# Where four tiles lie and who prepares the last norm: a one-core encoder block

## The chip, the core and the metric

The kernel runs on one core of a Trainium2 chip. The metric is the device time of one execution in microseconds (us), and of several executions the median. Engines are named as in the profile: PE (TensorE), DVE (VectorE), ACT (ScalarE), POOL (GpSimd), SP (SyncE, which here only issues DMAs).

## The reference

One layer on 1024 tokens of width 1024, in float32. Two mixers share an input projection: sparse attention (8 heads of 64, each query keeps the 256 best keys by an index score) and gated linear attention. Their outputs go through `w_out`, a residual and a first layer norm. Then 32 experts, of which each token takes two, a residual and a second layer norm.

```python
mix = jnp.concatenate([ya, yb], axis=-1) @ w_out[l]
h = layer_norm(DEEPNORM_ALPHA * h + mix, ln1_g[l], ln1_b[l])
ffn = hier_moe(h, ...)            # 32 experts, top 2 of one group of 8
h = layer_norm(DEEPNORM_ALPHA * h + ffn, ln2_g[l], ln2_b[l])
```

## The kernel before

**Projections.** x lies in SBUF as high and low halves (`xhi`, `xlo`), so that three fast matmuls make one float32 product. `load_w` brings each piece of `w_in` in as `wraw` and splits it into `whi` and `wlo`. The last projection is `values(1, ...)`: four matmul groups, each copied by ScalarE from PSUM into a tile `vs` (L687) and written by a DMA of GpSimd's queue to the DRAM tensor `d_av` (L688). The `vs` tiles take turns in buffers of two tags, `vs` and `wraw`.

**Attention.** For each of four head pairs and eight query blocks of 128 (item n = 8 * pair + block) and for both heads: PE makes scores `s` (L839), DVE adds the bias and takes the maximum into `Sm` (L844), ACT takes the exponential (L852), PE transposes `Sm` into PSUM `pt` (L863), and ACT or DVE copies that to SBUF as `PT` (L868, L866). A block later PE multiplies `PT` with the values into `ot` (L877). PE's order runs: scores of n, transposes of n-1, products of n-2. Every four blocks the sums' reciprocals are spread by POOL into `rb` (L910), transposed by PE (L885), copied by ACT into `R` (L887), multiplied by DVE (L888) and written to `d_mix` by SP (L889). The order on PE, ACT and DVE here is that of the code.

The SBUF pool `att` of `Sm`, `PT`, `rb`, `R` is opened where the projections' pools have been closed. A tile that is allocated over closed tiles waits for whatever last used the bytes, a DMA that reads them among it. A tag with `bufs=2` takes its place at its first two allocations, in the order in which the code asks.

**Experts.** 192 pieces of weights of 1 MB go through 13 slots, eight of the pool `big`, two in the score buffer `sc`, three more; SP issues each when its slot is free. `results` scales an expert's two output halves by the gate, one on ACT (L1404) and one on DVE (L1405), and an indirect DMA adds the rows to `d_y` (L1406). After the 32 experts a loop of 0 to 16 turns takes care of overfull experts; here it turns zero times, but all engines and DMAs meet in front of it (L1501).

**Last norm.** `last_norm` loads eight tiles `r` of `d_y` (L1560, SP), while PE spreads gain and shift over 128 partitions in four PSUM banks (L1332). [...] `LAST` has a word of three letters for each tile: first who takes the statistics (A: ACT with two passes, L1574 and L1577; D: DVE with `bn_stats`, L1583), then for each half who applies them (D: DVE alone, L1604 and L1605; P: ACT scales at L1607, then POOL multiplies and adds at L1612; G and S: DVE and POOL share, L1610 and L1612). The reciprocal root is POOL's (`rstd`, L498 and L499). SP writes the results (L1614, L1616).

Of the kernel before, what the change touches and what calls it, by code (L numbers as in the profile page):

```python
# [9 lines left out]
F32 = mybir.dt.float32  # L10
# [5 lines left out]
AF = mybir.ActivationFunctionType  # L16
OP = mybir.AluOpType
# [4 lines left out]
D = 1024  # L22
# [7 lines left out]
NE = 32  # L30
# [17 lines left out]
WORAW = 4  # L48


LAST = ("ADP", "DDD", "APP", "DDD", "ADD", "ADD", "ADD", "AGS")
WS = [(t + 1) * 128 for t in range(2, NT)]
SOFF = [int(v) for v in np.cumsum([0] + WS)]

# [110 lines left out]
class Kern:  # L165
# [514 lines left out]
    def values(self, g, w, tiles, queue=None):  # L680
        nc = self.nc
        queue = queue or nc.sync
        for t in tiles:

            vs = self.wpool.tile([128, 2, 2, 128], F32, name="vs", tag="wraw" if g and t > 2 else "vs", bufs=3 if g and t > 2 else 2)
            ps = yield from self.proj_n_steps(w, t)
            nc.scalar.copy(vs, ps.rearrange("p t (a b) -> p a t b", a=2))  # L687
            queue.dma_start(self.d_av[g][:, :, t:t + 2, :].rearrange("a p t c -> p a t c"), vs)  # L688
# [131 lines left out]
    def attention(self, p, before):  # L820

        nc = self.nc
        ident = self.c["ident"]
        items = [(hp, t) for hp in range(4) for t in range(NT)]
        st = {}

        def scores(n, hd):
            s = st[n]  # L830
            t, W = s["t"], s["W"]
            qq, kk, _ = s["loads"]
            lq = qq[:, hd, t * 128:(t + 1) * 128]
            ps = self.bank("s", [128, 2 * 512])
            cuts = [(0, W)] if W <= 512 else [(0, W // 2), (W // 2, W // 2)]
            for c, (c0, m) in enumerate(cuts):
                mm = max(m, 256)
                for a in range(2):
                    nc.tensor.matmul(ps[:, 512 * c:512 * c + mm], lq, kk[hd][:, a, c0:c0 + mm], start=a == 0, stop=a == 1)  # L839

            Sm = p.tile([128, T], F32, name="Sm", bufs=4)
            mx = p.tile([128, 1], F32, name="mx", bufs=4)
            m = cuts[0][1]
            nc.vector.tensor_tensor_reduce(  # L844
                Sm[:, :W].rearrange("p (c m) -> p c m", m=m), ps.rearrange("p (c m) -> p c m", m=512)[:, :len(cuts), :m],
                self.bias[t][:, :W].rearrange("p (c m) -> p c m", m=m), -0.125, -OUTSIDE, op0=OP.add, op1=OP.min, accum_out=mx)
            s["S"].append((Sm, mx))

        def weights(n, hd):
            s = st[n]  # L850
            Sm, mx = s["S"][hd]
            nc.scalar.activation(Sm[:, :s["W"]], Sm[:, :s["W"]], AF.Exp, bias=mx, scale=-1.0,  # L852
                                 accum_out=s["rec"][:, s["t"] % 4, hd:hd + 1])

        def turned(n, hd):
            s = st[n]
            t, P = s["t"], s["S"][hd][0]
            PT = p.tile([128, NT, 128], F32, name="PT", bufs=4)
            for b0 in range(0, t + 1, 4):
                nb = min(4, t + 1 - b0)  # L860
                pt = self.bank("pt", [128, 512])
                for b in range(nb):
                    nc.tensor.transpose(pt[:, 128 * b:128 * b + 128], P[:, 128 * (b0 + b):128 * (b0 + b) + 128], ident)  # L863
                o = PT[:, b0:b0 + nb, :].rearrange("p a b -> p (a b)")
                if b0 or (t < 4 and hd):
                    nc.vector.tensor_copy(o, pt[:, :128 * nb])  # L866
                else:
                    nc.scalar.copy(o, pt[:, :128 * nb])  # L868
            s["PT"].append(PT)

        def mixed(n):
            s = st.pop(n)
            t, v, ot = s["t"], s["loads"][2], s["ot"]
            for b in range(t + 1):
                for hd in range(2):
                    r = slice(64 * hd, 64 * hd + 64)
                    nc.tensor.matmul(ot[r, t % 4, :], v[:, b, r], s["PT"][hd][:, b, :], start=b == 0, stop=b == t)  # L877
            if t % 4 == 3:
                return s

        def shares(s):

            rp = self.bank("pt", [128, 4, 128])
            for i in range(4):
                nc.tensor.transpose(rp[:, i, :], s["rb"][:, 2 * i:2 * i + 2, :].rearrange("p a b -> p (a b)"), ident)  # L885
            R = p.tile([128, 4, 128], F32, name="R", bufs=2)
            nc.scalar.copy(R.rearrange("p a b -> p (a b)"), rp.rearrange("p a b -> p (a b)"))  # L887
            nc.vector.tensor_mul(R, R, s["ot"])  # L888
            nc.sync.dma_start(self.d_mix[s["t"] // 4][:, :, s["hp"], :].rearrange("t p q -> p t q"), R)  # L889

        rec = ot = done = None
        with self.tc.manual_schedule(engines={mybir.EngineType.PE, mybir.EngineType.Activation, mybir.EngineType.DVE}):
            for n in range(len(items) + 2):
                new, turn = n if n < len(items) else None, n - 1 if 0 < n <= len(items) else None
                if new is not None:
                    hp, t = items[n]
                    loads = before(n)
                    if t % 4 == 0:
                        rec = p.tile([128, 4, 2], F32, name="rec", bufs=2)
                    st[n] = {"hp": hp, "t": t, "W": 128 * (t + 1), "S": [], "PT": [], "rec": rec, "loads": loads}  # L900
                if turn is not None:
                    s = st[turn]
                    if s["t"] % 4 == 0:
                        ot = self.bank("ot", [128, 4, 128])
                    s["ot"] = ot
                    if s["t"] % 4 == 3:
                        rb = s["rb"] = p.tile([128, 8, 64], F32, name="rb", bufs=2)
                        rr = p.tile([128, 8], F32, name="rr", bufs=2)
                        nc.vector.reciprocal(rr, s["rec"].rearrange("p a b -> p (a b)"))
                        nc.gpsimd.tensor_copy(rb, rr.unsqueeze(2).to_broadcast([128, 8, 64]))  # L910
                for hd in range(2):
                    if new is not None:
                        scores(new, hd)
                    if turn is not None:
                        turned(turn, hd)
                    if new is not None:
                        weights(new, hd)
                over, done = done, mixed(n - 2) if n > 1 else None
                if over:
                    shares(over)  # L920
            shares(done)
# [415 lines left out]
    def expert_stream(self, cols, x, work):  # L1337


        nc = self.nc  # L1340
# [15 lines left out]
        def second(e, a, between=None):  # L1356
            ys = [self.bank("ot", [128, 512]) for _ in range(2)]
            product(a, ys, 4, 0)
            ahead()
            out = between() if between else None  # L1360
            product(a, ys, 4, 1)
            self.results(ys, cols(e))
            ahead()
            return out

# [2 lines left out]
        for e in range(NE):  # L1368
# [25 lines left out]
                x = self.rows_in(self.xg[(e + 1) % 2], cols(e + 1)[0]) if e else x1  # L1394
            if e:
                last = second(e - 1, ah, (lambda: self.turn_act(act)) if e == NE - 1 else None)
        second(NE - 1, last)

    def results(self, ys, cols):

        nc = self.nc
        tok, gate = cols
        y = self.ep.tile([128, D], F32, name="y", bufs=2)
        nc.scalar.activation(y[:, :512], ys[0], AF.Copy, scale=gate)  # L1404
        nc.vector.tensor_scalar(y[:, 512:], ys[1], gate, None, op0=OP.mult)  # L1405
        nc.gpsimd.indirect_dma_start(out=self.d_y, out_offset=bass.IndirectOffsetOnAxis(ap=tok.bitcast(U32), axis=0),  # L1406
                                     in_=y, in_offset=None, bounds_check=T - 1, oob_is_err=False, compute_op=OP.add)

# [145 lines left out]
    def last_norm(self, gain, shift):  # L1554
        nc = self.nc
        with self.pool("last") as p:
            rs, fs = [], []
            for t in range(NT):
                r = p.tile([128, D], F32, name="r", bufs=NT)
                nc.sync.dma_start(r, self.d_y[t * 128:(t + 1) * 128])  # L1560
                rs.append(r)


            both = p.tile([128, 2, D], F32, name="both")
            for i, ps in enumerate((gain, shift)):
                for k in range(2):
                    nc.scalar.copy(both[:, i, 512 * k:512 * k + 512], ps[k])

            def stats(t):

# [20 lines left out]
            for t in range(NT):  # L1591
# [9 lines left out]
                for k in range(2):  # L1601
# [4 lines left out]
                    else:  # L1606
                        nc.scalar.activation(r[:, s], r[:, s], AF.Identity, scale=f[:, 2:3], bias=f[:, 3:4])  # L1607
                        for i, (ps, op) in enumerate(((gain, OP.mult), (shift, OP.add))):
                            if kinds[k] == "GS"[i]:
                                nc.vector.tensor_tensor(r[:, s], r[:, s], ps[k], op=op)  # L1610
                            else:
                                nc.gpsimd.tensor_tensor(r[:, s], r[:, s], both[:, i, s], op=op)  # L1612
                    if t == NT - 1:
                        nc.sync.dma_start(self.out[t * 128:(t + 1) * 128, s], r[:, s])  # L1614
                if t < NT - 1:
# [15 lines left out]
```

## Time and profile before

| | |
|---|---|
| median of 3 runs | 1294.08 us (1291.38 to 1295.2) |
| the profiled execution | 1292.31 us, span 1290.5 us, mean granted clock 0.97 |
| busy in the span | PE 93%, DVE 80%, ACT 61%, POOL 31% |
| attention | first scores 393.24 us, first output product (L1057) 525.49 us |
| experts | last matmul ends at 1247.8 us |
| last norm | first load issued at 1259.42 us, last output issued at 1286 us |

The profile's page shows where PE is busy and which chain of work ended last. A list of waits names who held whom up; a timeline shows the instructions of a stretch. "x4" is a count of equal instructions merged into a row.

### The profile page before, as it was taken

Reading aid. Unit: us, or ns where it says so; the run is one execution under the profiler, and the core shown is the slowest. Engines: PE = TensorE matmul, PEld = TensorE weight load, DVE = VectorE, ACT = ScalarE, POOL = GpSimd, SP = SyncE. Lnnn points to the kernel's source line nnn. Section 1 sums busy time; section 2 is a strip of 40 time slices with the busy share of each in tenths; the row PEclk is TensorE's granted clock in tenths of the full one; section 3 lists DMA queues with packets and bytes.
Section 4 is the critical chain, followed back from the end, with each engine's and each line's share of the span. In section 5 each row is a group of like instructions: output and inputs, shape, how many; then the busy total and the mean of one; then the engine's idle time right before and its main releaser. Section 6 shows DMA issues by size and latency. Waiting matters only on the chain.

```text
span 1290.5 us, 19395 instructions
## 1 busy us (share of the span) xinstructions
PE 1204.2 (93%) x6926; PEld 1003.1 (78%) x6926; DVE 1028.6 (80%) x1657; ACT 792.8 (61%) x1112; POOL 394.5 (31%) x354
## 2 busy tenths in 40 slices
PE   6999999999996999999859999999999999999962
PEld 5979988877795888888747888888888888888851
DVE  4567897999993666477768999889998899889945
ACT  4378366665534667132257777777777777777835
POOL 2532642345753453011121321112221222122215
PEclk9999999999998999999979999999999999999985
DMA  7653544325468661874378999999999999999926
GB/s 257 163 180 99 191 156 126 112 61 143 105 186 242 190 170 58 308 278 164 131 271 313 375 372 367 382 368 360 380 365 369 351 361 357 352 356 353 321 44 260
DMA packets 133588, 322.61 MB, mean 250 GB/s; under 512 B 20953, under 2 KB 50546, under 8 KB 133490
## 3 DMA queue, kind: packets, MB, share of 16 engines
q1 hardware_dynamic: 109826, 280.92, 61.4%
q0 software_dynamic: 15168, 26.27, 8.1%
q10 hardware_dynamic: 8496, 14.16, 3.3%
q8 instruction: 55, 0.90, 0.3%
q14 instruction: 43, 0.35, 0.1%
HBM read 283.78 MB, written 54.26 MB: 262 GB/s over the span
## 4 chain that ended last, share of the span: by engine, by line
PE 73%; DVE 8%; DMA 6%; ACT 5%; another core or an unknown queue 3%; POOL 3%; issue 3%; SPq 0%; ACTq 0%; POOLq 0%; DVEq 0%
PE acc L1353 26%; PE ot L1353 13%; PE acc L1057 7%; PE acc L236 5%; PE acc L222 4%; PE pt L1420 3%; PE ot L877 3%; DVE eq L723 3%; PE s L839 2%; PE pt L863 2%; PE g L236 1%; DMA d_mix<-ym 1%; PE ot L1072 1%; PE g L222 1%
## 5 line engine op out<-in xcount | busy, mean ns | idle before, releaser
L181 DVE TENSOR_TENSOR elo<-big,ehi 128x2048 fp32r<-128x2048 f32 (+1 forms) x132 | 268.0, 2062 | 21.9 <-ACT ehi L180 20.2
L180 ACT CAST ehi<-big 128x2048 fp32r<-128x2048 f32 (+1 forms) x132 | 223.0, 1727 | 0.0
L1353 PE MATMUL acc<-ehi,xh 128*128 128x512 f32 x512 | 206.4, 403 | 2.0 <-ACT sg L1469 2.0
L1353 PE MATMUL acc<-ehi,xl 128*128 128x512 f32 x512 | 203.3, 397 | 0.0
L1353 PE MATMUL acc<-elo,xh 128*128 128x512 f32 x512 | 203.2, 397 | 0.0
L1427 POOL DMA_INDIRECT xg<-d_h,tok x32 | 36.8, 1151 | 360.8 <-PE pt L1420 360.3
L222 PE MATMUL acc<-big,whi 128*128 128x512 f32 (+1 forms) x384 | 120.3, 392 | 10.0 <-ACT big L180 10.0
L1406 POOL DMA_INDIRECT d_y<-y,tok x32 | 96.2, 3006 | 105.8 <-ACT ehi L180 50.2
L236 PE MATMUL acc<-whi,big 128*128 128x256 f32 x672 | 125.4, 286 | 0.0
L1353 PEld LDWEIGHTS acc<-ehi,xh 128*128 128x128 f32 x512 | 96.7, 189 | 24.5 <-ACT sg L1469 2.4
L1353 PEld LDWEIGHTS acc<-ehi,xl 128*128 128x128 f32 x512 | 96.6, 189 | 23.6 <-DVE xl L181 0.3
L1353 PEld LDWEIGHTS acc<-elo,xh 128*128 128x128 f32 x512 | 97.0, 189 | 22.0
L236 PEld LDWEIGHTS acc<-whi,big 128*128 128x128 f32 x672 | 105.6, 192 | 1.8 <-issue 1.0
L723 DVE TENSOR_SCALAR_CACHE_REDUCE eq<-sc,cand 128x384 bf16<-128x384 f32 (+1 forms) x124 | 100.5, 810 | 7.0 <-POOL sc L735 4.6
L1353 PE MATMUL ot<-ehi,ah 128*128 128x512 f32 x256 | 104.1, 407 | 0.4 <-ACT ah L180 0.4
L181 DVE TENSOR_TENSOR elo<-slot,ehi 128x2048 fp32r<-128x2048 f32 (+1 forms) x46 | 95.5, 2102 | 7.8 <-ACT ehi L180 7.3
L1353 PE MATMUL ot<-ehi,al 128*128 128x512 f32 x256 | 101.5, 397 | 0.0
L1353 PE MATMUL ot<-elo,ah 128*128 128x512 f32 x256 | 101.4, 396 | 0.0
L753 ACT ACTIVATE sn<-sc,cand 128x896 bf16<-128x896 f32 (+1 forms) x62 | 68.0, 1097 | 46.5 <-DVE cand L749 36.5
L236 PE MATMUL acc<-wlo,big 128*128 128x256 f32 x336 | 95.8, 285 | 0.0
L222 PEld LDWEIGHTS acc<-big,whi 128*128 128x128 f32 x384 | 72.5, 193 | 25.1 <-ACT big L180 10.0
L1057 PE MATMUL acc<-wohi,m 128*128 128x512 f32 x256 | 86.0, 405 | 0.0
(297 smaller groups left out, 2601.6 us busy)
## 6 DMA issues: line engine op xcount, KB each, us to landing
big<-we SPq DMA_DIRECT2D x79, 1024.0 KB, 15.8
big<-wf SPq DMA_DIRECT2D x40, 1024.0 KB, 20.2
slot<-we SPq DMA_DIRECT2D x26, 1024.0 KB, 14.0
sc<-we SPq DMA_DIRECT2D x20, 1024.0 KB, 20.2
slot<-wf SPq DMA_DIRECT2D x16, 1024.0 KB, 23.2
wraw<-wi SPq DMA_DIRECT2D x52, 256.0 KB, 3.2
sc<-wf SPq DMA_DIRECT2D x8, 1024.0 KB, 10.5
raw<-xT SPq DMA_DIRECT2D x8, 512.0 KB, 6.9
```

The costliest lines, as they stand in the source:

```text
L180: nc.scalar.copy(hi, src)
L181: (lo_eng or nc.vector).tensor_tensor(lo, src, hi.bitcast(F32), op=OP.subtract)
L222: nc.tensor.matmul(ps[:m, :n], l[:, j, c0:c0 + m], r[:, j % 2, t0:t0 + n], start=(j == 0 and a == 0), stop=(j == 7 and a == 2))
L236: nc.tensor.matmul(ps[:, i, :], l[:, j % 2, s], r[:, j, :], start=(j == 0 and a == 0), stop=(j == 7 and a == 2))
L723: nc.vector.tensor_scalar(gtt[:, :WS[i]], x, v, 0.0, op0=op, op1=OP.add, accum_out=cnt[:, i:i + 1])
L753: nc.scalar.activation(jnk[:, :WS[i]], y[i], AF.Sign, bias=c, accum_out=cnt[:, i:i + 1])
L877: nc.tensor.matmul(ot[r, t % 4, :], v[:, b, r], s["PT"][hd][:, b, :], start=b == 0, stop=b == t)
L1057: nc.tensor.matmul(ps, l[:, j, :], w[:, j, s], start=(j == 0 and a == 0), stop=(j == 7 and a == 2))
L1353: nc.tensor.matmul(o, x[:, jj, :], w[:, j, s], start=(jj == 0 and a == 0), stop=(jj == n - 1 and a == 2))
L1406: nc.gpsimd.indirect_dma_start(out=self.d_y, out_offset=bass.IndirectOffsetOnAxis(ap=tok.bitcast(U32), axis=0), in_=y, in_offset=None, bou ...
L1420: self.last_mm = nc.tensor.transpose(pt[:, 128 * i:128 * i + 128], src[:, 128 * (b + i):128 * (b + i) + 128], self.c["ident"])
L1427: self.last_gather = nc.gpsimd.indirect_dma_start(out=xg, out_offset=None, in_=self.d_h, in_offset=bass.IndirectOffsetOnAxis(ap=tok.bitcas ...
```

## The change

Six edits in three stages. (1) `values(1)` writes into one tile `whole` under the tag `whi`, in place of four `vs`. (2) In attention `rb` and `R` take the flat shape 128x512, and their two places each are asked for first, before `Sm` and `PT`. (3) For the last but one expert ACT scales both output halves. (4) Gain and shift for POOL come by two broadcast DMAs into slot 8 (in `sc`), which SP issues behind the last weights; the four copies to `both` go. (5) The eight loads of `r` are issued by SP and ACT in turn. (6) Tile 3's statistics move from DVE to ACT.

```diff
-LAST = ("ADP", "DDD", "APP", "DDD", "ADD", "ADD", "ADD", "AGS")
+LAST = ("ADP", "DDD", "APP", "ADD", "ADD", "ADD", "ADD", "AGS")
...
+        whole = self.wpool.tile([128, 4, 2, 2, 128], F32, name="whole", tag="whi", bufs=2) if g else None
         for t in tiles:
-            vs = self.wpool.tile([128, 2, 2, 128], F32, name="vs", tag="wraw" if g and t > 2 else "vs", bufs=3 if g and t > 2 else 2)
+            vs = whole[:, t // 2] if g else self.wpool.tile([128, 2, 2, 128], F32, name="vs", bufs=2)
...
-            R = p.tile([128, 4, 128], F32, name="R", bufs=2)
+            R = p.tile([128, 512], F32, name="R", bufs=2).rearrange("p (a b) -> p a b", b=128)
...
+        for name in ("rb", "R"):
+            for _ in range(2):
+                p.tile([128, 512], F32, name=name, bufs=2)
...
-                        rb = s["rb"] = p.tile([128, 8, 64], F32, name="rb", bufs=2)
+                        rb = s["rb"] = p.tile([128, 512], F32, name="rb", bufs=2).rearrange("p (a b) -> p a b", b=64)
...
-            self.results(ys, cols(e))
+            self.results(ys, cols(e), e == NE - 2)
...
+        self.both = self.slots[8]
+        for i in range(2):
+            nc.sync.dma_start(self.both[:, i], self.I["l2"][i:i + 1].to_broadcast([128, D]))
         second(NE - 1, last)
...
-        nc.vector.tensor_scalar(y[:, 512:], ys[1], gate, None, op0=OP.mult)
+        if act:
+            nc.scalar.activation(y[:, 512:], ys[1], AF.Copy, scale=gate)
+        else:
+            nc.vector.tensor_scalar(y[:, 512:], ys[1], gate, None, op0=OP.mult)
...
-                nc.sync.dma_start(r, self.d_y[t * 128:(t + 1) * 128])
+                (nc.sync, nc.scalar)[t % 2].dma_start(r, self.d_y[t * 128:(t + 1) * 128])
...
-            both = p.tile([128, 2, D], F32, name="both")
-            for i, ps in enumerate((gain, shift)):
-                for k in range(2):
-                    nc.scalar.copy(both[:, i, 512 * k:512 * k + 512], ps[k])
...
-                                nc.gpsimd.tensor_tensor(r[:, s], r[:, s], both[:, i, s], op=op)
+                                nc.gpsimd.tensor_tensor(r[:, s], r[:, s], self.both[:, i, s], op=op)
```

PE's instructions stand in the same order before and after. What moves is best seen at three places. The names of semaphores in the rows: DMAHW0 to 7 are the eight that the DMAs of SP's and ACT's queues use in turn, DMASW those of POOL's queue; the engines' own bear their names. (The changed file's lines lie 1 to 12 further down.)

DVE at the start of attention, before; `Sm` are the scores, `mx` their maximum, `PT` the first transposed block that DVE copies:

```order
L844 ISA Sm,mx<-s,bias_92 128x128 [waits PE_49]
L844 ISA mx 128x1
L844 ISA Sm,mx<-s,bias_92 128x128 [waits PE_49]
L844 ISA mx 128x1
L1032 MEMSET g_6050 128x8
L1244 COPY val<-K 128x2 x6
L844 ISA Sm,mx<-s,bias_92 128x256 [waits PE_49]
L844 ISA mx 128x1
L844 ISA Sm,mx<-s,bias_92 128x256 [waits PE_49]
L844 ISA mx 128x1
L866 COPY PT<-pt 128x128 [waits DMAHW1_49,DMAHW4_49,DMAHW0_49,DMAHW5_49,DMASW7_49,DMAHW6_49,DMASW1_49,PE_49]
```

The same place on DVE in the change:

```order
L845 ISA Sm,mx<-s,bias_92 128x128 [waits DMAHW4_49,DMAHW6_49,DMAHW1_49,DMAHW7_49,DMAHW0_49,PE_49]
L845 ISA mx 128x1
L845 ISA Sm,mx<-s,bias_92 128x128 [waits DMAHW5_49,DMAHW4_49,DMAHW6_49,DMAHW1_49,PE_49]
L845 ISA mx 128x1
L1037 MEMSET g_6051 128x8
L1249 COPY val<-K 128x2 x6
L845 ISA Sm,mx<-s,bias_92 128x256 [waits PE_49]
L845 ISA mx 128x1
L845 ISA Sm,mx<-s,bias_92 128x256 [waits PE_49]
L845 ISA mx 128x1
L867 COPY PT<-pt 128x128 [waits DVE_49,PE_49]
```

The first `PT` copy has lost its waits for DMAs, those of POOL's queue (DMASW) among them; the first two `Sm` have gained waits for DMAs of SP's and ACT's queues.

POOL around the writes of `d_av`, before, and behind them the first `rb` copies:

```order
L688 DMA d_av_68<-vs 128x2x256 [waits Activation_49]
L282 DMA d_k_72<-rp_2932 4x32x512 [waits Pool_49]
L688 DMA d_av_68<-vs 128x2x256 [waits Activation_49] x3
L910 COPY rb<-rr 128x512 [waits DMASW7_49,DVE_49]
L910 COPY rb<-rr 128x512 [waits DVE_49]
```

The same rows in the change:

```order
L689 DMA d_av_68<-whole 128x2x256 [waits Activation_49]
L282 DMA d_k_72<-rp_2932 4x32x512 [waits Pool_49]
L689 DMA d_av_68<-whole 128x2x256 [waits Activation_49] x3
L915 COPY rb<-rr 128x512 [waits DMASW2_49,DMASW3_49,DMASW1_49,DMASW7_49,DVE_49,PE_49]
L915 COPY rb<-rr 128x512 [waits DVE_49]
```

The waits for all four writes of `d_av` now stand at the first `rb`, which lies over `whole`.

ACT from the last norm's first instruction on, before; `jnk` is the scrap output of a statistics pass:

```order
L1567 COPY both<-acc 128x512 [waits PE_49]
L1574 ACTIVATE jnk,f<-r 128x1024 [waits DMAHW3_49]
L1577 ACTIVATE jnk,f<-r,f 128x1024 [waits Activation_49]
L1567 COPY both<-ot 128x512 [waits PE_49]
L1574 ACTIVATE jnk,f<-r 128x1024 [waits DMAHW5_49]
L1567 COPY both<-acc 128x512 [waits PE_49]
L1607 ACTIVATE r<-r,f 128x512 [waits Activation_49,Pool_49]
L1577 ACTIVATE jnk,f<-r,f 128x1024 [waits Activation_49]
L1567 COPY both<-ot 128x512 [waits PE_49]
L1574 ACTIVATE jnk,f<-r 128x1024 [waits DMAHW7_49]
```

And in the change:

```order
L1572 DMA r<-d_y 128x1024 x4
L1580 ACTIVATE jnk,f<-r 128x1024 [waits DMAHW5_49]
L1583 ACTIVATE jnk,f<-r,f 128x1024 [waits Activation_49]
L1580 ACTIVATE jnk,f<-r 128x1024 [waits DMAHW7_49]
L1580 ACTIVATE jnk,f<-r 128x1024 [waits DMAHW0_49,Activation_49]
L1583 ACTIVATE jnk,f<-r,f 128x1024 [waits Activation_49]
L1613 ACTIVATE r<-r,f 128x512 [waits Pool_49]
L1580 ACTIVATE jnk,f<-r 128x1024 [waits DMAHW1_49,Activation_49]
L1583 ACTIVATE jnk,f<-r,f 128x1024 [waits Activation_49]
L1613 ACTIVATE r<-r,f 128x512 [waits Pool_49]
```

Four copies are gone from ACT, four DMA issues stand at its head, and the two passes over tile 3 come in.

## Rows read from the trace of the kernel before

**Rows 1.** Waits from 380 to 430 us: who waited for whom, sum, times, longest.

```profile
PE pt L863 <- DVE PT L866: 8.9, 1, 8.9
```

**Rows 2.** Timeline, attention's start: start, length (us), what [idle before <- releaser].

```profile
393.67 0.29 DVE L844 CUSTOM_DVE_ANT_0 Sm<-s,bias 128x128 f32<-128x128 f32 x1 [4.46 <-PE s L839]
...
396.10 2.18 POOL L688 DMA_DIRECT2D d_av<-vs  x3
...
397.19 0.19 ACT L852 ACTIVATION_READ_ACCUMULATOR Sm<-Sm,mx 128x1 f32 x1
404.58 0.33 SPq L813 DMA_DIRECT2D big<-d_av  x1
...
406.11 0.29 DVE L866 COPY PT<-pt 128x128 f32<-128x128 f32 x1 [9.37 <-DMA d_av<-vs]
...
406.55 0.66 PE L863 MATMUL pt<-K,Sm 128*128 128x128 f32 x2 [8.87 <-DVE PT L866]
...
409.33 0.63 SPq L813 DMA_DIRECT2D big<-d_av  x1
...
411.73 0.85 PE L839 MATMUL s<-kq,kq 128*128 128x320 f32 x4
```

**Rows 3.** Busy time by stretch: us, PE, PEld, DVE, ACT, POOL, granted clock, DMA share, GB/s.

```profile
408.00:410.00 2.00, 2.00 (x7) 1.61 (x8) 0.96 (x3) 0.82 (x3) 0.00 (x0) 0.50 0.94 278
...
436.00:438.00 2.00, 2.00 (x17) 1.58 (x17) 1.38 (x5) 1.16 (x4) 1.77 (x4) 1.00 0.30 88
...
460.00:480.00 20.00, 19.93 (x192) 16.56 (x192) 12.39 (x33) 13.55 (x34) 15.23 (x20) 1.00 0.63 155
```

**Rows 4.** Timeline of PE, the second head pair's first blocks.

```profile
428.63 0.51 PE L839 MATMUL s<-big 128*128 128x256 f32 x2
...
436.89 0.38 PE L863 MATMUL pt<-K,Sm 128*128 128x128 f32 x2
...
440.38 0.86 PE L839 MATMUL s<-big 128*128 128x320 f32 x4
```

**Rows 5.** Line L688: what its DMAs took to land.

```profile
DMA to landing us min/median/max: 9.9/10.0/10.1
```

**Rows 6.** Line L196: count, duration ns, first to last start.

```profile
L196 SPq DMA_DIRECT2D wraw<-wi x52: 367/383/776, 0.7 to 350.2; - x52
```

**Rows 7.** The page's DMA issues: last, median us to landing.

```profile
big<-d_k SPq DMA_DIRECT2D x12, 256.0 KB, 7.1
```

**Rows 8.** The chain that ended last: start, length.

```profile
423.10 0.59 PE pt L885 x4
```

**Rows 9.** Busy time by stretch, in the experts.

```profile
1140.00:1160.00 20.00, 20.00 (x94) 16.23 (x93) 17.25 (x13) 15.48 (x13) 4.14 (x2) 1.00 1.00 365
```

**Rows 10.** Timeline, from the last weights to the last tile.

```profile
1205.03 13.35 SPq L979 DMA_DIRECT2D big<-wf  x4
...
1250.71 1.54 POOL L1406 DMA_INDIRECT d_y<-y,tok  x1 [5.42 <-DMA d_y<-y,tok]
...
1263.19 1.06 ACT L1574 ACTIVATE jnk<-r 128x1024 f32<-128x1024 f32 x1 [0.48 <-DMA r<-d_y]
...
1264.46 1.29 DVE L1583 BATCH_NORM_STATS2 bnst<-r 128x6 f32<-128x512 f32 x2 [15.86 <-DMA r<-d_y]
...
1280.77 0.19 POOL L498 TENSOR_SCALAR f<-f 128x1 f32<-128x1 f32 x1
...
1281.90 1.52 ACT L1607 ACTIVATE r<-r,f 128x512 f32<-128x512 f32 x2 [1.84 <-POOL f L1600]
```

**Rows 11.** Tile r: count, duration ns min/median/max, first and last start.

```profile
L1560 SPq DMA_DIRECT2D r<-d_y x8: 354/440/533, 1259.4 to 1262.8; - x8
...
L1574 ACT ACTIVATE jnk<-r x6: 1048/1056/1062, 1263.2 to 1276.6; 128x1024 f32<-128x1024 f32 x6
...
L1577 ACT ACTIVATE jnk<-r,f x6: 1140/1146/1151, 1264.4 to 1278.8; 128x1024 f32<-128x1024 f32 x6
```

**Rows 12.** Tile both: the same columns.

```profile
L1567 ACT COPY both<-acc x2: 573/580/587, 1262.1 to 1267.0; 128x512 f32<-128x512 f32 x2
```

More of the change, by code (lines that the diff above doesn't have):

```diff
@@ L1396, in expert_stream, with results @@
                 last = second(e - 1, ah, (lambda: self.turn_act(act)) if e == NE - 1 else None)
+        self.both = self.slots[8]
+        for i in range(2):
+            nc.sync.dma_start(self.both[:, i], self.I["l2"][i:i + 1].to_broadcast([128, D]))
         second(NE - 1, last)
-    def results(self, ys, cols):
+    def results(self, ys, cols, act=False):
         nc = self.nc
```

## The prediction

> **What bounds the kernel now.** I read the page's slices first, then the waits, the timeline of the stretch that these point to, the busy time by stretch, and last the DMA landings and the end of the kernel.
>
> From attention's middle to the last expert PE is the bound: it is busy 19.93 of 20 us in a stretch of attention [rows 3] and 20.00 of 20 in the experts [rows 9], both at granted clock 1.00. So a microsecond that PE loses or wins before that comes out at the end of the experts, unless a transfer takes it.
>
> At attention's start PE does lose time. The largest wait of PE there comes once, 8.9 us, for DVE's copy of `pt` into `PT` [rows 1]. The timeline says why [rows 2]: that copy starts at 406.11 and was idle for 9.37 us before, until a DMA landed that writes `d_av` from `vs`. GpSimd's queue issued the last three of these from 396.10 on, and a DMA of that line takes 9.9 to 10.1 us to land [rows 5]: issued at 396.10, the first is down at about 406.1. Nothing in the computation ties `PT` to `d_av`. `PT` lies over the bytes of `vs`, so its first writer waits until these have been read. Scores, maximum and exponential were done long before: the last read-out of the exponential that the next transposes need ends at 397.19 + 0.19 = 397.38, and PE's transposes go on at 406.55 after 8.87 us of idle time [rows 2].
>
> [...]
>
> The end is another regime. PE is out of it; ACT's chain of statistics passes sets the pace, from the first pass over tile 0 at 1263.19 to the wait that ends at 1281.90 for the root that POOL makes for the last tile [rows 10].
>
> **The change part by part.**
>
> *Edits 1 and 2, where tiles lie.* The first copy of `PT` on DVE waits for DVE and PE only; the waits for GpSimd's writes of `d_av` now stand at POOL's first `rb`, which is needed by the first reciprocals' transposes, four blocks in. At PE the next thing due is then the exponential: the transposes go at 397.38 in place of 406.55, which is **-9.17 us**. Bounds: nothing if a wait as long takes its place, 9.17 if none does; I take the whole, because the rows that follow need nothing that is issued later than the old weights and the first head pair's loads.
>
> The clock: from these transposes to the scores of block 4 it is 411.73 - 406.55 = 5.18 us [rows 2]; the same piece of the second pair takes 440.38 - 436.89 = 3.49 us [rows 4], and that includes the reciprocals' transposes, which the first lacks. So at least 1.69 is lost to the lower clock, and at most half of 5.18, 2.59. I take **-2.0**, near the lower end, because the first piece may be held by DVE and ACT here and there, which run at their own pace.
>
> What the first two `Sm` gain, waits for DMAs of SP's and ACT's queues, I cost at nothing: the tiles under them were last filled by weight loads of `wraw`, and the last of the 52 is issued at 350.2 [rows 6], 43 us before the first `Sm` at 393.67 [rows 2]. What POOL gains, the wait at `rb`, ends when the writes have landed. They are issued by 396.10 + 2.18 = 398.28 and take at most 10.1 [rows 2, 5], so the last lands by 408.4 and `rb` follows. The transposes of the first `rb` start at 423.10 [rows 8], 11.2 us earlier at most in the change, that is 411.9: 3.5 us to spare. Queued behind `rb` on POOL is nothing that PE needs before that.
>
> *Edit 3, one expert's scaling.* ACT takes over a half of the last but one expert. The second scatter of the end starts after 5.42 us of waiting for the first to land [rows 10], so a half that ends earlier or later moves the first scatter and the end with it; a like copy of 512 columns by ACT takes 0.58 [rows 12]. I take 0, with 0.6 either way.
>
> *Edit 4, gain and shift by two DMAs.* SP's last weights are all issued by 1205.03 + 13.35 = 1218.4, and the scatters keep the kernel going until past 1250.71 + 1.54 [rows 10]. Two more loads behind them have over 30 us to land. They are hidden; without this cover they would stand before the loop's meeting point with about the 7.1 us of a usual load [rows 7]. Of the four copies that go, one stands ahead of the first statistics pass, where ACT waits for tile 0 anyway; three stand between passes, 3 x 0.58 = -1.74 [rows 12].
>
> *Edit 6, tile 3's statistics.* Two passes more on ACT, 1.06 + 1.15 = +2.21 [rows 11], together with the three copies +0.47. DVE is freed and POOL's roots for other tiles come at other moments: at the end ACT is idle for 1.84 us, from 1280.06, but POOL begins the last tile's root only at 1280.77 because it is busy with another [rows 10]. Without that queue 0.6 is saved. Edits 4 and 6 come to -0.1, which I call 0. Bounds: +2.2, if the copies filled gaps, and -0.7, if the passes overlap with waiting.
>
> *Edit 5, two queues for the eight loads.* SP issues eight loads with a median of 440 ns each, the first at 1259.4 [rows 11]; tile 0 is there 3.8 us later, at 1263.19, tile 1 at 1264.46, when DVE starts on it [rows 10]. ACT's own four issues, 4 x 0.44 = 1.8 us, are over by 1261.3, before tile 0 lands, and so hidden. [...] I take **+0.6**, the middle.
>
> *Sum*, on the profiled execution's own 1292.31 us: -9.17 - 2.0 + 0 + 0.6 = -10.57, so 1281.7. The median of the runs, 1294.08, lies 1.77 above that execution; the difference taken from it gives 1283.5.
>
> **The rivals.**
>
> *Two tiles land as one.* Tile 0 arrives only when tile 1 does: +1.27 in place of +0.6, 1284.2. For it speaks that the loads are of equal size and start together; against it, that nothing here shows two such queues side by side. [...]
>
> *The next head pair's loads become the wait.* The scores of block 8 start at 428.63 and read a `big` [rows 4]; in the change they are due at 428.63 - 11.2 = 417.4. SP issues the last loads of that group at 409.33 [rows 2], and a load takes 7.1 us [rows 7], which makes 416.4: one microsecond to spare. The DMA engines are 94% busy at 408 [rows 3]; if landing takes the 10.0 of rows 5, it is 419.3, and PE waits 1.9 us: 1285.4. Against it: the scores need the first loads of the group, not the last.
>
> *No gain.* The change doesn't do what it says: ACT's first `PT`, which the rows of the order do not show, still waits for a late transfer, and PE with it. Then only the tail's +0.6 is left, 1294.7. Against it: the tag's places serve both engines in turn, and DVE's first copy no longer names a DMA.
>
> *Slower.* The wait moves one step ahead, to the first `Sm`, if the semaphores that it shares with later transfers make it wait for these. SP itself waits for a landing until 404.58 [rows 2]. With the first `Sm` at 404.58 in place of 393.67, the transposes follow as now 397.38 - 393.67 = 3.71 us later, at 408.3: 1.7 after 406.55, with the tail +2.3, 1296.4; with the landing of 406.11 it is 409.8, 1297.9. It decides from a landing after 406.55 - 3.71 = 402.8 on. Against it: the loads that it names are 43 us old.
>
> **How the numbers follow.** My forecast 0.62; two tiles as one 0.15; next loads 0.12; no gain 0.06; slower 0.05. What a measurement of this kernel can tell from no change is 0.3%, 3.9 us. The first three are faster: 0.89. No gain lies within 0.3%, and of the slower case, at +2.3 to +3.8, a bit under half: same 0.08, slower 0.03. The forecast's own range: clock -2.59 to -1.69, edits 4 and 6 -0.7 to +2.2, edit 5 0 to 1.27, edit 3 0.6 either way; all at their good ends give 1281.0, all at the bad ones 1287.3. Medians of three runs move by 1 to 2 us themselves (1291.38 to 1295.2 before), so the range reaches from 1279.5 to 1288.5; the cases outside it hold about 0.11 and the noise the rest.
>
> **What would show it.** Right: no DMA in front of the first `PT` copies; transposes near 397.4; granted clock 1.00 from 400 to 412; the first output product near 525.49 - 11.2 = 514; the last expert's end near 1236.6; POOL's `rb` waiting for `d_av`. For the tail: the stretch from the first load of `r` to the first statistics pass, 3.77 us before, at 4.4 (5.0 by the first rival); from there to the last root about as long as before. Wrong: a DMA in front of `Sm` or of ACT's `PT`, a PE wait between 410 and 420 for `big`, or the lower clock in spite of steady work.

## The result, and the profile after

The changed kernel takes 1280.8 us (median of 4 runs, 1278.77 to 1281.3) against 1294.01 before (4 runs); the ratio is 0.9902, 95% interval 0.9886 to 0.9919. Run again beside another kernel it was 1281.14 against 1290.55, ratio 0.9915 (0.9888 to 0.9941). The forecast was 1283.5 with a range of 1279.5 to 1288.5. The two profiled executions, 1292.31 and 1281.19 us, lie 11.12 apart; the sum that the prediction made on that footing was 10.57. By the medians the gain is 13.2 us here and 9.4 us in the second comparison, so the forecast lies between the two.

The timeline of the changed kernel at attention's start answers to [rows 2]:

```profile
393.96 0.29 DVE L845 CUSTOM_DVE_ANT_0 Sm<-s,bias 128x128 f32<-128x128 f32 x1 [5.47 <-PE s L840]
...
395.11 2.18 POOL L689 DMA_DIRECT2D d_av<-whole  x3
...
395.80 0.28 DVE L867 COPY PT<-pt 128x128 f32<-128x128 f32 x1
...
396.85 0.38 PE L864 MATMUL pt<-K,Sm 128*128 128x128 f32 x2
...
399.90 0.85 PE L840 MATMUL s<-kq,kq 128*128 128x320 f32 x4
...
407.81 0.61 POOL L915 COPY rb<-rr 128x512 f32<-128x512 f32 x1 [10.52 <-DMA d_av<-whole]
```

DVE's first `PT` copy (L867) has no idle time and no DMA ahead of it, and the idle time before the first `Sm` (L845) ends with PE's scores, not with a DMA. The transposes that started at 406.55 start at 396.85. The wait for `d_av` is still there, 10.52 us of idle time, but POOL has it, and the transposes of `rb` come at 411.20, 2.8 us after that copy ends. The busy time by stretch, the columns as in [rows 3], shows the other half:

```profile
408.00:410.00 2.00, 2.00 (x18) 1.72 (x15) 1.93 (x4) 1.43 (x2) 0.42 (x1) 1.00 0.99 299
```

The granted clock is 1.00 where it was 0.50, at about the same load on the DMA engines (a share of 0.99, before 0.94). It is 1.00 in every stretch of 2 us from 396 to 414. The first output product starts at 513.48 us, where 514 was forecast, and the last expert's matmuls end at 1236.3, where 1236.6 was.

The end of the changed kernel, from the scatters to the last root, answers to [rows 10]:

```profile
1229.51 0.59 ACT L180 CAST ah<-pt 128x512 fp32r<-128x512 f32 x1 [1.57 <-PE ot L1358]
...
1231.54 1.54 POOL L1418 DMA_INDIRECT d_y<-y,tok  x1 [10.99 <-ACT y L1415]
...
...
1246.78 2.14 SPq L1572 DMA_DIRECT2D r<-d_y  x4
1246.93 2.16 ACTq L1572 DMA_DIRECT2D r<-d_y  x4
1250.63 1.06 ACT L1580 ACTIVATE jnk<-r 128x1024 f32<-128x1024 f32 x1 [14.31 <-DMA r<-d_y]
...
1253.94 1.06 ACT L1580 ACTIVATE jnk<-r 128x1024 f32<-128x1024 f32 x1 [0.89 <-DMA r<-d_y]
...
1270.79 1.52 ACT L1613 ACTIVATE r<-r,f 128x512 f32<-128x512 f32 x2 [1.60 <-POOL f L1606]
```

ACT now waits a second time for a tile (0.89 us, until 1253.94), and from its first pass to the scaling by the last root it takes 20.16 us, before 1281.90 - 1263.19 = 18.71. The forecast had this part as long as before, and the first pass 4.4 us after the first load; it came 3.85 after.

Between two marks in each trace the parts can be told apart better than by whole times. "Attention" is from the first scores to the first output product (both from the timeline; before, it has the product at 525.32, the chain that ended last at 525.49), "scatter" from ACT's last split of activations (`ah`) to the first of the last two scatters, "load" from the first load of `r` to the first statistics pass, "norm" from there to the end of the span. The four lengths, in us, are of one profiled execution of each kernel; the ratio is of all its runs:

```
kernel            attention  scatter  load   norm   ratio to before (95%)
before              132.08    2.71    3.77   27.31
changed             119.95    2.03    3.85   28.77   0.9902 (0.9886-0.9919)
change_again        124.33    2.03    4.16   28.62   0.9915 (0.9888-0.9941)
memory_only         121.47    2.70    3.64   27.37   0.9904 (0.9882-0.9925)
tail_only           132.37    2.03    4.03   28.72   0.9998 (0.9981-1.0015)
whole_only          137.95    2.71    3.59   27.30   1.0020 (1.0003-1.0037)
places_only         134.72    2.71    3.63   27.33   1.0025 (1.0009-1.0041)
busy_wait           129.23    2.70    3.49   27.41   0.9986 (0.9968-1.0004)
edit4_undone        119.92    2.03    3.89   29.74   0.9919 (0.9894-0.9945)
edit5_undone        119.96    2.03    3.64   28.77   0.9916 (0.9887-0.9946)
edit6_undone        119.96    2.02    4.19   27.78   0.9901 (0.9875-0.9927)
edits5_6_undone     123.78    2.03    3.60   26.50   0.9925 (0.9899-0.9951)
values_by_dve       120.59    2.03    3.53   26.55   0.9896 (0.9878-0.9914)
```

### The profile page after: what moved, and what is told of

Its sections match the earlier page's. It is cut to its first block, busy times and chain, and to the rows that moved or that the text cites. A ratio compares the mean times of both kernels' runs of the same rounds, so it can differ in the third digit from the quotient of the medians.

```text
span 1279.4 us, 19391 instructions
## 1 busy us (share of the span) xinstructions
PE 1201.7 (94%) x6926; PEld 1001.3 (78%) x6926; DVE 1025.0 (80%) x1652; ACT 793.2 (62%) x1113; POOL 392.6 (31%) x354
## 4 chain that ended last, share of the span: by engine, by line
PE 73%; DVE 8%; DMA 8%; ACT 4%; another core or an unknown queue 3%; issue 2%; POOL 1%; SPq 0%; ACTq 0%; POOLq 0%; DVEq 0%
PE acc L1358 25%; PE ot L1358 12%; PE acc L1062 7%; PE acc L236 6%; PE acc L222 4%; DVE eq L724 3%; PE pt L1432 3%; PE ot L878 3%; PE s L840 3%; PE pt L864 2%; DMA slot<-we 2%; PE g L222 2%; PE g L236 1%; DMA xg<-d_h,tok 1%
```

## The experiments

**The two halves of the change.** First the memory edits alone on the kernel before:

```diff
+        whole = self.wpool.tile([128, 4, 2, 2, 128], F32, name="whole", tag="whi", bufs=2) if g else None
...
+        for name in ("rb", "R"):
+            for _ in range(2):
+                p.tile([128, 512], F32, name=name, bufs=2)
```

> The kernel before with the two memory edits alone (whole, and the places of rb and R asked for first). Theory (the gain is all the wait of PT for the writes of d_av and the clock that follows it): the second transposes of block 1 start about 9.7 us earlier against the first scores than before, the piece from there to the scores of block 4 takes about 3.0 us in place of 5.18, granted clock 1.00 from 400 to 412, first output product near 513.5, execution 11.5 to 12.5 us under before, ratio about 0.991. Rival (a third of the gain is in the tail's edits): 8 us under before. Tail from the first load of r to the end of the span as before, 31 us.

Measured 1281.66 against 1291.7, ratio 0.9904: the gain of the whole change, as far as the two intervals can tell. The rival's 8 us would be 0.9938, outside the interval. The transposes and the scores of block 4 in its trace:

```profile
399.00 0.38 PE L864 MATMUL pt<-K,Sm 128*128 128x128 f32 x2
...
402.05 0.85 PE L840 MATMUL s<-kq,kq 128*128 128x320 f32 x4
```

The scores of block 4 come 3.05 us after the second transposes of block 1, as expected, and the granted clock is 1.00 from 396 to 414. The transposes come 4.50 us after the first scores in place of 13.31, so 8.8 us earlier and not 9.7. The first output product is at 515.97, not 513.5, and the gain by the medians 10.0 us, not 11.5 to 12.5. The norm takes 27.37, as before.

The rest of the change without these two, `whole` and the requests taken out again:

> The changed kernel without its two memory edits, so that only the scaling by ACT, the broadcast loads, the two load queues and ACT's statistics of tile 3 are left. Theory: the wait of 8.9 us at the transposes and the clock of 0.50 behind it are back; from the last split of the activations (al) to the end of the span about 0.4 us more than before: the first scatter 0.7 earlier, the last norm from the first statistics pass to the last root 1.4 longer. Execution 1293 to 1296, no difference that can be told. Rival (the tail's edits bring what is missing between my -10.6 and the measured -13.2): about 1291.5.

Measured 1293.08 against 1291.7, ratio 0.9998 (0.9981 to 1.0015): no difference, with room for about 2 us either way. PE's wait is back in its trace, 8.98 us, and so is the clock of 0.50 from 408 to 410. So the four edits of the tail are no visible part of the gain; in the norm they cost 1.4 us, at the scatter they win 0.7. From the last `ah` to the end of the span it takes 49.41 us, before 49.46, where 0.4 more was expected; but memory_only, without these edits, takes 48.50, so this stretch moves by a microsecond by itself.

**Each memory edit alone.** Edit 1 without edit 2:

```diff
+        whole = self.wpool.tile([128, 4, 2, 2, 128], F32, name="whole", tag="whi", bufs=2) if g else None
...
-            vs = self.wpool.tile([128, 2, 2, 128], F32, name="vs", tag="wraw" if g and t > 2 else "vs", bufs=3 if g and t > 2 else 2)
+            vs = whole[:, t // 2] if g else self.wpool.tile([128, 2, 2, 128], F32, name="vs", bufs=2)
```

> The kernel before with edit 1 alone: the values in one tile under the tag of whi, rb and R take their places where they did. Theory (where tiles lie decides who waits): the first Sm now lies over whole and waits for all four writes of d_av, until about 407; behind it stand maximum, exponential and transposes, 2.9 us to the second transposes of block 1, so these start near 410 in place of 406.55, and the clock is low behind them as before. Slower than before by 3 to 4.5 us, about 1297.5. Rival (each of the two memory edits brings its half): about 1288.

And edit 2 without edit 1, the requests for `rb` and `R` in front and their flat shape:

> The kernel before with edit 2 alone: rb and R take their places first, the values stay in four tiles. Theory: Sm, rb and R are shifted against vs; the first Sm waits for the third write of d_av, the second Sm for the fourth, which land near 407; so as with edit 1 alone the wait stands one step earlier in the chain, second transposes of block 1 near 410, slower than before by 3 to 4.5 us, about 1297.5. Rival (half the gain each): about 1288.

Both are slower than before: ratios 1.0020 (1.0003 to 1.0037) and 1.0025 (1.0009 to 1.0041), so 2.6 and 3.2 us where 3 to 4.5 were expected. In the timeline of the first:

```profile
410.53 0.29 DVE L845 CUSTOM_DVE_ANT_0 Sm<-s,bias 128x128 f32<-128x128 f32 x1 [19.22 <-DMA d_av<-whole]
...
410.89 0.80 PE L840 MATMUL s<-kq,kq 128*128 128x256 f32 x2 [15.70 <-DVE mx L845]
```

and in the timeline of the second:

```profile
406.07 0.29 DVE L844 CUSTOM_DVE_ANT_0 Sm<-s,bias 128x128 f32<-128x128 f32 x1 [17.86 <-issue]
...
406.42 0.80 PE L839 MATMUL s<-kq,kq 128*128 128x256 f32 x2 [12.54 <-DVE mx L844]
...
410.09 0.63 PE L863 MATMUL pt<-K,Sm 128*128 128x128 f32 x2
```

The same DMAs now stand in front of the first `Sm`, a step that comes before `PT`. PE stands still for 15.70 and 12.54 us in place of 8.87. (In the second trace no event is shown as the releaser of `Sm`. The third write of `d_av`, which was expected to be it, was issued at about 396.3, an estimate from POOL's busy time, 1.80 us of 396 to 398 and nothing behind that; `Sm` starts at 406.07, about 9.7 us later, where such a write took 9.9 to 10.1 us to land before.) 410.09 is what was expected. In the first trace the transposes come at 414.09, 4 us later than expected: `Sm` waits for the last of the four writes, which was issued at 398.52, where before it was 397.56. The two writes ahead of it took 11.0 and 11.1 us to land, where before they took 10.0; the landing of the last is not shown, and the start of `Sm` at 410.53 puts it up to 12.0 us after the issue. So the two edits don't add up: each by itself moves the wait to a place that is worse, and only together they move it to `rb`, where there is slack.

**The clock by itself.** The kernel before, with PE kept busy inside its wait:

```diff
+FILL = 32
...
+        def filler(s):
+            qq, kk, _ = s["loads"]
+            ps = self.bank("ot", [128, 512])
+            for _ in range(FILL):
+                nc.tensor.matmul(ps, qq[:, 0, :128], kk[0][:, 0, :512], start=True, stop=True)
...
+                    if n == 2 and hd:
+                        filler(st[n])
```

> The kernel before with 32 more matmuls of 128x512 between the scores of block 2 and the transposes that wait for PT, into the bank of products that is free there (their result is not used): about 7.5 us of work inside the wait of 8.9. Theory (the lower clock comes from PE standing still): the transposes start where they did, near 406.5, but the granted clock stays at 1.00 and the piece from there to the scores of block 4 takes 3.0 to 3.3 us in place of 5.18; execution 1.5 to 2.5 us under before. Rival (the clock falls for another reason, as the many transfers or the change of stage): the piece stays at 5.2, execution the same, or above before if the matmuls last longer than the wait.

PE's timeline in it, and the busy time by stretch:

```profile
397.22 7.42 PE L896 MATMUL ot<-kq,kq 128*128 128x512 f32 x32
406.00 0.41 PE L864 MATMUL pt<-K,Sm 128*128 128x128 f32 x2 [1.35 <-DVE PT L867]
...
409.43 0.85 PE L840 MATMUL s<-kq,kq 128*128 128x320 f32 x4
```

```profile
408.00:410.00 2.00, 2.00 (x19) 1.52 (x18) 1.46 (x5) 1.84 (x6) 0.00 (x0) 1.00 1.01 315
```

The wait for `PT` ends at 406.00, before at 406.55; the clock stays at 1.00 in every stretch from 396 to 414, with the DMA engines as busy as before (1.01, before 0.94); the piece, from these transposes to the scores of block 4, takes 3.43 us in place of 5.18. So 7.4 us of useless work win 1.75 us here. The ratio, 0.9986 (0.9968 to 1.0004), has the size that was expected but does not exclude none; the trace settles it. The clock fell because PE stood still: in the kernel before it stood from 397.7 to 406.5 and the granted clock was 0.50 from 402 to 410; here it stood for 1.35 us at most.

**The edits of the tail, one at a time,** from the changed kernel. Their ratios (0.9901 to 0.9919, the changed kernel's 0.9902) do not tell them apart by time; what follows is read from one trace each.

```diff
-LAST = ("ADP", "DDD", "APP", "ADD", "ADD", "ADD", "ADD", "AGS")
+LAST = ("ADP", "DDD", "APP", "DDD", "ADD", "ADD", "ADD", "AGS")
```

> The changed kernel with tile 3's statistics on DVE again. Theory (ACT's passes set the last norm's pace): two passes of 2.2 us less on ACT, from the first pass to the last 15.2 to 15.6 us in place of 17.33, from the first pass to the end of the span 26.7 to 27.2 in place of 28.77; execution 1.5 to 2 us under the changed kernel. Rival (DVE is as long as ACT, so that the moved work comes back there): from the first pass to the end 28 to 29, no gain.

From ACT's first pass to the start of its last it takes 15.20 us in place of 17.33, as expected; but the norm is shorter by 0.99 only (27.78). The other half is spent in POOL's queue:

```profile
1269.15 1.52 ACT L1613 ACTIVATE r<-r,f 128x512 f32<-128x512 f32 x2 [2.71 <-POOL f L1606]
```

The last tile's root stands behind the roots of other tiles there, and ACT waits 2.71 us for it in place of 1.60. Neither theory is right by itself.

```diff
-                (nc.sync, nc.scalar)[t % 2].dma_start(r, self.d_y[t * 128:(t + 1) * 128])
+                nc.sync.dma_start(r, self.d_y[t * 128:(t + 1) * 128])
```

> The changed kernel with all eight loads of r issued by SP. Theory (two queues bring tiles in pairs, so that tile 2, which ACT wants second, comes later): tile 2 lands 6 us after the first load's issue in place of 6.9, ACT's second first-pass starts 2.4 to 2.8 us after the first in place of 3.31, the tail is 0.5 to 0.9 shorter. Rival (two queues bring the tiles earlier as a whole): the first pass starts later, and the tail is up to 1 us longer.

ACT's second tile starts 2.55 us after its first in place of 3.31, and the load is 0.2 shorter. The norm as a whole stays at 28.77, because in this run DVE, which ends later, holds POOL's last addition:

```profile
1269.79 1.26 POOL L1618 TENSOR_TENSOR r<-r,sc 128x512 f32<-128x512 f32 x1 [0.57 <-DVE r L1616]
```

```diff
-        self.both = self.slots[8]
-        for i in range(2):
-            nc.sync.dma_start(self.both[:, i], self.I["l2"][i:i + 1].to_broadcast([128, D]))
...
+            self.both = p.tile([128, 2, D], F32, name="both")
+            for i, ps in enumerate((gain, shift)):
+                for k in range(2):
+                    nc.scalar.copy(self.both[:, i, 512 * k:512 * k + 512], ps[k])
```

> The changed kernel with gain and shift copied from PSUM by ACT again in place of the two broadcast loads. Theory: three copies of 0.47 to 0.58 stand among ACT's passes again, of which one fits into the wait of 0.89 for tile 2; from the first pass to the last 18.2 to 18.8 us in place of 17.33, execution about 1 us above the changed kernel. Rival (the copies fill gaps anyway): no difference, 17.3.

The norm is 0.97 longer (29.74), and from the first pass to the last it takes 18.31, as expected. By these traces the broadcast loads are the one edit in the norm that pays.

Edits 5 and 6 undone together, with the changed kernel beside it:

> The changed kernel with the loads of r all on SP and tile 3's statistics on DVE. Theory (both edits cost something in the tail, and what they cost adds up as far as POOL and DVE allow): the second first-pass 2.5 us after the first, from the first pass to the last 14.3 to 14.8 us in place of 17.33, but the last root waits in POOL's queue behind others, so from the first pass to the end 27.0 to 27.8 in place of 28.77; execution 1 to 1.5 us under the changed kernel, too little to be sure of by the time alone. Rival (POOL's queue takes all of it back): 28.5 or more from the first pass to the end, the time of the changed kernel.

> The changed kernel once more, beside the next run on the same chip. Both theories: ratio to before 0.990 to 0.992, from the first statistics pass to the end of the span 28.7 us.

The norm takes 26.50 us, 2.27 less than in the changed kernel, a gain a little larger than expected, where undoing edit 6 alone gave 0.99 and edit 5 alone nothing. That each gain was held up by what the other edit left in the queues is my reading, not shown. The whole time doesn't show the 2.27 either (medians 1282.47 and 1281.14): the six runs of each kernel spread over 6.8 and 9.4 us. Both profiled executions lose about 4 us in attention against the first trace of the changed kernel, and part of that spread may come from there. The timeline of change_again says where they are lost:

```profile
395.84 0.62 ACT L180 CAST so_hi<-rp 128x512 fp32r<-128x512 f32 x1 [2.05 <-DMA d_k<-so_hi]
...
397.05 2.05 ACT L688 COPY whole<-acc 128x512 f32<-128x512 f32 x4 [0.60 <-ACT so_hi L180]
...
397.69 0.53 PEld L840 LDWEIGHTS s<-kq,kq 128*128 128x128 f32 x4 [2.72 <-ACT whole L688]
```

The copies of the values stand on ACT behind a split that waits for a DMA. PE needs the bank that they free for its second scores and stands 2.5 us; after that the clock is at 0.50 from 400 to 402 here too. (The row of PE's matmul itself names a load, `big<-d_k`, as what came last; the weight load in front of it and the chain of work through this stretch name ACT's copies, and in edits5_6_undone, where PE stands 1.79 us at the same place, both rows name them.) So I gave these copies to DVE, idle there, on top of edits5_6_undone:

```diff
-            nc.scalar.copy(vs, ps.rearrange("p t (a b) -> p a t b", a=2))
+            (nc.vector.tensor_copy if g else nc.scalar.copy)(vs, ps.rearrange("p t (a b) -> p a t b", a=2))
```

> The changed kernel with the loads of r on SP, tile 3's statistics on DVE, and the four copies of the values from PSUM into whole by DVE in place of ACT; in the trace of change_again PE stood 2.5 us at the second scores because ACT made the first copy late, behind a split (so_hi) that waited for a DMA. Theory (with the wait of PT gone, this is what is late next, in some executions): no PE wait of over 0.5 us between the first scores and the first transposes; the first Sm up to 0.7 us later than in the changed kernel, as the last copy now stands ahead of it on DVE; first output product at most 121 us after the first scores; execution 1 to 3 us under edits5_6_undone, about 1279.5. Rival (the copies on DVE hold the first Sm as long as ACT's held the scores): the time of edits5_6_undone or of the changed kernel, 1281 to 1282.5.

1278.15 us against 1291.75, ratio 0.9896 (0.9878 to 0.9914), the lowest median, and the least spread of the kernels that ran six times or more (1277.39 to 1280.76). PE's longest wait from the first scores to the first transposes is 0.52 us, for DVE's maximum. Its interval overlaps those of the changed kernel and of edits5_6_undone, so the order by time is likely and not shown. Nor did its trace meet the bad case: ACT's split starts 0.71 us before the first scores, in change_again 1.06 behind them. That the smaller spread comes from the moved copies is likely and not shown.

## Why the prediction was right, step by step

*The wait.* Right in cause and place: -9.17 forecast. From the first scores to the second transposes of block 1 it is 396.85 - 393.53 = 3.32 us, before 406.55 - 393.24 = 13.31, so -9.99. The 0.8 in between is ACT: its copies of the values started at 393.21 before and at 392.22 in the changed trace, and the exponential behind them with them. That is the piece that varies from run to run. In the eight traces with both memory edits it is 3.32 us four times, and 3.58, 4.50, 6.35 and 7.39, so the wait brought from 5.9 to 10.0 us. The successor was right where it is short: the exponential. In the three longest it is ACT's copies of the values: they start 0.19, 1.55 and 2.27 us behind the first scores, in the changed trace 1.31 us ahead of them. The prediction did not weigh them. That the forecast came so near in the first pair of traces is luck to that extent.

*The clock.* -2.0 forecast, on the 0.50 that [rows 3] show from 408 to 410; -2.13 measured (399.90 - 396.85 = 3.05 in place of 5.18), and by busy_wait a consequence of standing still. DVE and ACT kept their pace meanwhile: DVE's `Sm` of 128x512 at 409.13 takes 0.69 us and ACT's exponential of 128x384 at 407.84 takes 0.60, in the changed trace at 1.00 they take 0.69 and 0.62. In change_again the lower clock is back, 0.50 from 400 to 402, after PE stood 2.51 us. In edits5_6_undone, after 1.79 us, the second transposes of block 1 take 0.63 us, where they take 0.38 in the changed trace at 1.00 and 0.66 before at 0.50.

*What takes the wait's place.* The first two `Sm` did not wait for the loads of `wraw`, and `rb` had 2.8 us to spare where 3.5 were forecast (1.0 to 3.7 in the eight traces with both memory edits). The loads of the next pair held nothing up: PE is busy 9.94 of 10 us from 410 to 420. The rival "slower" was weighed for the wrong reason, semaphores shared with later transfers, but it had the right place, and a price not far off, for a neighbour of this change: each memory edit alone puts the wait at the first `Sm`, with the transposes at 410.09 and 414.09 where the rival said 408.3 to 409.8.

*Edit 3.* Forecast 0, with 0.6 either way; -0.68 at the first scatter, alike in all traces (2.70 or 2.71 without it, 2.02 or 2.03 with it). Missed: on DVE the half stood behind a split of the activations, on ACT it follows the other half at once.

*Edits 4 and 6.* Called 0; together with the wait for tile 2 the norm grew by 1.46. Two terms were mis-sized. Each of the three copies holds up the next instruction by 0.47, not 0.58, and undoing edit 4 costs 0.97, not 1.74, as one copy then falls into the wait for tile 2. The queue of roots in POOL gave back 0.24 (1.84 to 1.60), not 0.6. A third term, the wait of 0.89 us for tile 2, the sum did not have at all. In edit 6 alone, 2.13 of ACT's time is 0.99 of the norm.

*Edit 5.* +0.6 forecast at the first pass. No run shows that term; in its place the runs show, with one queue, 3.49 to 3.77 us in 8 traces, mean 3.61, and with two queues 3.85 to 4.19 in 5, mean 4.02; so +0.41 by the means. The second queue brought the first tile no sooner but 0.4 later. More of the loss comes one tile later: ACT starts tile 2 3.31 us after tile 0 in place of 2.55. What edit 5 costs the norm hangs on edit 6: nothing beside it (28.77 either way), 1.28 without it (27.78 and 26.50). The rival by which both tiles come at once (5.0) went too far.

*The tail as a whole.* Its errors have both signs, so +0.6 came out near the sum of the first pair of traces: 28.77 - 27.31 = +1.46 in the norm, -0.68 at the scatter, +0.08 at the load, and from the first of the last two scatters to the first load, past the second scatter and the loop's meeting point, -0.43; together +0.43. Luck, and twice over. The terms were wrong, and nothing shows that the -0.43 is the edits' work: the same stretch takes 14.39 to 15.67 us in the five traces without the tail's edits and 14.63 to 15.24 in the three with all four. From the last `ah` to the end of the span the five take 47.99 to 49.46 us, the kernel before the longest, and the three 49.41 to 49.89. By the means that is +1.1.

*The whole.* In the first pair of traces the parts close: -9.99 for the wait, -2.13 for the clock, +0.29 as attention starts later, +0.31 between the first output product and the last `ah`, +0.43 in the tail, together -11.1, the difference of the two spans.

## What to carry to other kernels

Here a tile placed over a closed one inherited its last reader, a DMA that took 9.9 to 10.1 us to land. Before moving such a tile, list every instruction that will be first on those bytes, and choose the one with slack: here a wait moved one step up a chain cost 2.6 to 3.2 us more than it did, and moved to `rb` nothing that shows. Ask of a standstill of TensorE whether it counts twice: here it cost 8.87 us for itself and 2.13 for the granted clock of 0.50 behind it. A queue that gains work at the end is to be asked what else is in it: undoing two edits together gave more than the sum of undoing each. And a sum that comes out right is to be checked term by term.

## What the runs showed of the hardware that was not expected

The same writes of GpSimd's queue that took 9.9 to 10.1 us to land before took 10.2 to 11.0 in the changed kernel and 11.0 to 11.1 in whole_only, there up to 12.0 for the last by the start of `Sm`; a forecast that hangs on such a landing should carry one to two microseconds for it, an estimate from these numbers. And 7.4 us of matmuls whose result nobody reads made PE's next piece take 3.43 us in place of 5.18. Two load queues in place of one made tile 0 come 0.4 us later by the means (3.61 and 4.02 us from the first load to the first pass), and tile 2 late enough for ACT to wait 0.89 us.
